# Last norm of a post-norm decoder layer: three quarter products moved behind the statistics, 44 idle products on TensorE, a register load pinned, the last output halves split

## The chip, the cores and the metric

The kernel runs on one core of one Trainium2 chip. The metric is the device time of one execution in microseconds (us), of which the median of several runs counts. The profile is that of one execution; its span runs from the first to the last instruction on the core.

## The reference, cut to what matters

One decoder layer over 256 tokens of width 1024. A mixer and a first layer norm come first and are not touched. Then a mixture of 16 experts, of which each token takes two, and the second layer norm, which is the end of the program:

```python
h = moe(x, w_router, router_bias, w_gate[l], w_up[l], w_down[l])
x = layer_norm(DN_ALPHA * x + h, ln2_g[l], ln2_b[l])

def layer_norm(x, g, b):
    mu = jnp.mean(xf, -1, keepdims=True)
    var = jnp.mean(jnp.square(xf - mu), -1, keepdims=True)
    y = (xf - mu) * lax.rsqrt(var + LN_EPS) * g + b
```

With y the row before the norm, r = 1/sqrt(var + eps) and m = -mu*r, the output is (y*g)*r + (m*g + b). The kernel computes y*g on VectorE, m*g + b as a small product on TensorE, and joins the two in one VectorE operation.

## The kernel before, in words

**Experts.** `moe_round` takes the 16 experts in eight pairs, numbered 0 to 7 in `pr`. For each pair the 64 token slots of each expert are multiplied by the gate and up weights (L1290), turned (L1361), and the pair before is multiplied by its down weights (L1301) and scattered back to the token rows (L1310, L1311) into four PSUM tiles `py` that gather all pairs. The weights come from HBM through a ring of buffers, issued on SyncE (L946). Pair 7 is the last: after its down weights have arrived nothing more is read from HBM.

**The last pair.** L1385 to L1390 handle the down product of pair 7 in four column quarters of 256. For each quarter: 16 products `pd` (L1301), a copy to a rounded part on ScalarE (L100) and the remainder on VectorE (L101), four scattering products `py` (L1310, L1311), the sum with the row, `y_sb` (L1377, one operation for each half of the tokens, n = 0 and 1), and the partial statistics (L1379). `last` calls `gained(i - 1)` first: the products y*g of the quarter before (L1270, two operations of 128x256).

**The branch.** Where some expert has more than 64 tokens, further rounds are needed. The count was put into an integer, and `nc.values_load` (L1351) loads it into a register of every engine. After `moe_round` each engine compares its register and branches (L1396): with the count at zero it goes through a short block, which waits on the engine's own semaphore and adds to it what the rounds left out would have added, and then jumps behind the loop's body, which holds one more copy of the experts' code. TensorE's part of that body is by far the longest.

**The last norm.** L1402 joins the statistics, L1404 takes the root on ScalarE, L1405 calls `gained(3, (0,))`, L1406 to L1410 make r and the columns of m, L1414 turns them with two TensorE transposes into `pn`, L1416 copies them to `nmT` on ScalarE, `gained(3, (1,))` follows. Then for each half c of the columns and each half n of the tokens: a product `pgb` of 5 rows by 512 columns (L1422, the first instruction that needs `nmT`), the joining operation `yo` (L1424), and the output transfer on SyncE's queue (L1425). L1449 is the end of the program, with its waits for the transfers.

**Order.** The order on each engine is a planner's, made ahead of time. `P` and `K` are one function, `keep_in_program_order`: it adds an edge to an instruction that puts it behind the instruction written just before it for the same engine. An instruction without the edge is placed where the planner likes, as far as its data allows. SyncE's order is that of the program. The register loads of L1351 have no edge. Each engine works through its instructions in order, TensorE's weight loads (PEld) aside, which run ahead of its products.

## Time and profile before

| | us |
|---|---|
| median of 3 runs | 617.74 (616.12 to 619.96) |
| the profiled execution | 617.43 |
| its span | 615.6 |
| granted TensorE clock, mean over the span | 0.989 |
| TensorE, products: busy | 587.5 (95%) |
| VectorE busy | 323.8 (53%) |
| ScalarE busy | 253.4 (41%) |

Of the profiled execution's 617.43 us, 1.8 us lie outside its span. The shares are averages over the whole span; the change lies in its last 2.5%, from about 600 us on, where TensorE is idle more than half of the time. [...]

### The profile page before, as it was taken

To read this page: it belongs to the slowest core of one execution; us is meant where nothing else is said; L and a number is where in the kernel's file an instruction comes from. 1 tells how busy PE (TensorE), PEld (TensorE's weight loads), DVE (VectorE), ACT (ScalarE), POOL (GpSimd) and SP (SyncE) were. 2 spreads that over 40 slices of the span, in tenths; PEclk is the share of its full clock that TensorE was granted. 3 is DMA by queue.
4 is the path that set the end of the run, shared out by engine and by line. 5 is a ranking of instruction groups with operands and counts; after the bars stand their busy time and mean duration, and the time that the engine had idled before them with its cause. 6 is when DMAs were issued, how large, how long until landed. Compare 5 with 4: busy or idle time off the path is not lost. (4 is left out here: it accounts for less than half of the span.)

```text
span 615.6 us, 10554 instructions
## 1 busy us (share of the span) xinstructions
PE 587.5 (95%) x4231; PEld 459.4 (75%) x4231; DVE 323.8 (53%) x651; ACT 253.4 (41%) x413; POOL 18.8 (3%) x53
## 2 busy tenths in 40 slices
PE   6999999999988999999999999999999999999992
PEld 5999999989978999999999999633533534444351
DVE  3798887677465986555565655542210300121245
ACT  5556664563469784443434544311211211021121
POOL 3000010100111000000000000000000000000000
PEclk9999999999999999999999999999999999999996
DMA  7877453742220436588998895889999999999941
GB/s 207 230 224 196 137 162 128 210 133 71 70 70 8 156 123 201 187 301 327 357 365 300 264 404 184 304 328 399 417 414 409 414 415 409 416 417 407 417 168 71
DMA packets 86380, 160.43 MB, mean 261 GB/s; under 512 B 9963, under 2 KB 56161, under 8 KB 86326
## 3 DMA queue, kind: packets, MB, share of 16 engines
q1 hardware_dynamic: 86198, 159.44, 71.5%
q8 instruction: 35, 0.57, 0.4%
q0 software_dynamic: 128, 0.26, 0.2%
q14 instruction: 19, 0.16, 0.1%
HBM read 158.50 MB, written 1.18 MB: 259 GB/s over the span
## 5 line engine op out<-in xcount | busy, mean ns | idle before, releaser
L133 DVE TENSOR_TENSOR wlo<-raw,whi 128x1024 fp32r<-128x1024 f32 (+1 forms) x106 | 125.9, 1200 | 53.3 <-ACT whi L129 52.6
L129 ACT CAST whi<-raw 128x1024 fp32r<-128x1024 f32 x102 | 105.9, 1048 | 101.4 <-PE pcm L275 34.8
L271 PE MATMUL pcm<-xh,whi 128*128 128x256 f32 x512 | 126.1, 284 | 2.3 <-ACT whi L131 1.5
L275 PE MATMUL pcm<-xl,whi 128*128 128x256 f32 x512 | 125.0, 282 | 0.0
L271 PEld LDWEIGHTS pcm<-xh,whi 128*128 128x128 f32 x512 | 97.4, 190 | 3.2 <-ACT whi L131 1.9
L275 PEld LDWEIGHTS pcm<-xl,whi 128*128 128x128 f32 x512 | 97.4, 190 | 0.1
L280 PE MATMUL pcm<-xh,wlo 128*128 128x256 f32 x512 | 72.5, 283 | 0.3 <-DVE wlo L133 0.2
L280 PEld LDWEIGHTS pcm<-xh,wlo 128*128 128x128 f32 x512 | 65.8, 190 | 0.8 <-DVE wlo L133 0.7
L101 DVE TENSOR_TENSOR dd<-pd,dd 128x512 fp32r<-128x512 f32 (+1 forms) x18 | 11.4, 632 | 95.3 <-ACT dd L100 95.3
L1301 PE MATMUL pd<-ew,sh 128*64 128x512 f32 (+1 forms) x288 | 56.8, 546 | 0.7 <-ACT sh L1362 0.7
L1290 PE MATMUL wu<-ew,xg 128*64 128x512 f32 x256 | 57.4, 593 | 0.0
L1290 PE MATMUL wg<-ew,xg 128*64 128x512 f32 x256 | 56.7, 595 | 0.6 <-issue 0.6
L1301 PEld LDWEIGHTS pd<-ew,sh 128*64 128x64 f32 x288 | 20.4, 137 | 35.1 <-issue 30.3
L1290 PEld LDWEIGHTS wu<-ew,xg 128*64 128x64 f32 x256 | 18.5, 137 | 36.2 <-issue 34.7
L1290 PEld LDWEIGHTS wg<-ew,xg 128*64 128x64 f32 x256 | 18.1, 137 | 33.5 <-issue 32.4
L271 PE MATMUL ptm<-whi,xh 128*128 128x256 f32 x128 | 32.6, 287 | 0.0
L271 PE MATMUL pbr<-yth,whi 128*128 128x256 f32 x128 | 32.1, 284 | 0.0
L275 PE MATMUL pbr<-ytl,whi 128*128 128x256 f32 x128 | 32.0, 282 | 0.0
L273 PE MATMUL ptm<-whi,xl 128*128 128x256 f32 x128 | 31.6, 281 | 0.0
L100 ACT CAST dd<-pd 128x512 fp32r<-128x512 f32 (+1 forms) x18 | 9.7, 539 | 46.3 <-PE pd L1301 46.3
L1207 ACT ACTIVATE xg<-pxg,gbp 128x128 f32<-128x128 f32 x32 | 13.3, 456 | 36.7 <-DVE xg L1206 35.8
L1341 DVE SCALAR_TENSOR_TENSOR sh<-wu,cw,sh 128x512 f32<-128x512 f32 x8 | 6.0, 751 | 37.9 <-PE wu L1290 37.8
(421 smaller groups left out, 887.5 us busy)
## 6 DMA issues: line engine op xcount, KB each, us to landing
raw<-in_w_in_dram SPq DMA_DIRECT2D x39, 1024.0 KB, 5.3
ew<-in_w_gate_dram SPq DMA_DIRECT2D x64, 512.0 KB, 9.8
ew<-in_w_up_dram SPq DMA_DIRECT2D x64, 512.0 KB, 9.6
ew<-in_w_down_dram SPq DMA_DIRECT2D x64, 512.0 KB, 9.8
raw<-in_w_branch_dram SPq DMA_DIRECT2D x8, 1024.0 KB
raw<-in_w_out_dram SPq DMA_DIRECT2D x4, 1024.0 KB
x<-in_x_dram SPq DMA_DIRECT2D x4, 256.0 KB, 5.3
raw<-in_w_in_dram SPq DMA_DIRECT2D x2, 512.0 KB
```

The lines of the kernel that those rows point to most:

```text
L100: A.copy(hi, ps)
L101: V.tensor_tensor(lo, ps, hi.bitcast(F32), op=OP.subtract)
L129: A.copy(hi, src)
L133: V.tensor_tensor(lo[:, c], src[:, c], hi[:, c].bitcast(F32), op=OP.subtract)
L271: T.matmul(o, sh(k), mh(k), start=first and k == 0, stop=False)
L273: T.matmul(o, sl(k), mh(k), start=False, stop=False)
L275: T.matmul(o, sh(k), ml(k), start=False, stop=False)
L280: T.matmul(o, sl(k), mh(k), start=False, stop=last and k == kt - 1)
L1207: A.activation(xg[1][:, 2 * kg + k, :], ps[kg][:, k, 128:256], AF.Identity, scale=g_, bias=b_)
L1290: P(T.matmul(p[r, :], xg[pr][:, k, r], W[pr, (nm, e, k // 2)][:, k % 2, :], start=k == 0, stop=k == 7))
L1301: P(T.matmul(p[r, :], hT[:, k, r], W[pr, ("wd", e, k)][:, 0, c0:c1], start=k == 0, stop=k == 3))
L1341: V.scalar_tensor_tensor(sg, pu, cw[pr // 2][:, pr % 2:pr % 2 + 1], sg, op0=OP.mult, op1=OP.mult)
```

## The change: what it does

Four edits. The product y*g of quarter 0 stays in `last`; those of quarters 1 and 2 leave it, and quarter 1 takes the place behind the statistics that quarter 3 had, with quarters 2 and 3 whole after the copy to `nmT`. Behind the last scattering product, 44 products of 128x256 in bfloat16 are added on TensorE; their result is never read. The second VectorE operation on the norm's weights in pair 7 gets the edge that keeps it behind the VectorE instruction written before it, which is that engine's register load. The last two of the four joining operations are cut in two halves of 256 columns, each with a transfer of its own.

```diff
-                    V.tensor_scalar(raw, raw, sgn[:, 1:2], None, op0=OP.mult)
+                    K(V.tensor_scalar(raw, raw, sgn[:, 1:2], None, op0=OP.mult))
...
         def last(c0, c1, dd, i):
 
-            if i:
-                gained(i - 1)
+            if i == 1:
+                gained(0)
...
         last(*cuts[-1], dd[0], len(cuts) - 1)
+        if first:
+            idle = pt("idle", (128, 2, 128))
+            for _ in range(44):
+                P(T.matmul(idle, selz[:, 1, 0:1].to_broadcast([128, 128]), stri[:, None, :].to_broadcast([128, 2, 128]),
+                           start=True, stop=True))
...
-    gained(3, (0,))
+    gained(1, (0,))
...
-    gained(3, (1,))
+    gained(1, (1,))
+    gained(2)
+    gained(3)
     for c in range(2):
         for n in range(2):
-            cs = slice(512 * c, 512 * c + 512)
             p = pt("pgb", (128, 512))
-            P(T.matmul(p, nmT[:, n, :], lnq[1][:, cs], start=True, stop=True))
-            y = yo[n][:, cs]
-            K(V.scalar_tensor_tensor(y, y, st2[:, n, 1:2], p, op0=OP.mult, op1=OP.add))
-            Q.dma_start(out[0, n * 128:(n + 1) * 128, cs], y)
+            P(T.matmul(p, nmT[:, n, :], lnq[1][:, 512 * c:512 * c + 512], start=True, stop=True))
+            for c0, c1 in ((0, 512),) if c + n < 2 else ((0, 256), (256, 512)):
+                y = yo[n][:, 512 * c + c0:512 * c + c1]
+                K(V.scalar_tensor_tensor(y, y, st2[:, n, 1:2], p[:, c0:c1], op0=OP.mult, op1=OP.add))
+                Q.dma_start(out[0, n * 128:(n + 1) * 128, 512 * c + c0:512 * c + c1], y)
```

## Rows read from the trace of the kernel before

**Rows 1.** The chain of waits that ended last, in order of time: start in us, length in us, what.

```profile
605.51 0.05 DVEq L1396
605.56 0.51 issue
606.07 0.40 DVE st L1402 x2
...
607.46 0.14 issue
607.60 0.60 PE pn L1414 x2
...
608.27 0.37 ACT nmT L1416
...
608.69 0.80 PE pgb L1422
...
609.51 0.89 DVE yo L1424 x2
```

**Rows 2.** VectorE's instructions in order of time: start, length, line and operation, out<-in and shapes, count; in brackets the idle time before and what ended it.

```profile
581.19 0.69 DVE L101 TENSOR_TENSOR dd<-pd,dd 128x512 fp32r<-128x512 f32 x1 [15.48 <-ACT dd L100]
...
600.98 0.75 DVE L1270 TENSOR_TENSOR yo<-y_sb,gall 128x256 f32<-128x256 f32 x2
...
601.65 0.75 DVE L1377 TENSOR_TENSOR y_sb<-py,y_sb 128x256 f32<-128x256 f32 x2
602.32 0.74 DVE L1379 BATCH_NORM_STATS2 bs<-y_sb 128x6 f32<-128x256 f32 x2
602.98 0.74 DVE L1270 TENSOR_TENSOR yo<-y_sb,gall 128x256 f32<-128x256 f32 x2
603.64 0.74 DVE L1377 TENSOR_TENSOR y_sb<-py,y_sb 128x256 f32<-128x256 f32 x2
604.30 0.74 DVE L1379 BATCH_NORM_STATS2 bs<-y_sb 128x6 f32<-128x256 f32 x2
606.07 0.39 DVE L1402 BATCH_NORM_AGGREGATE st<-bs 128x2 f32<-128x24 f32 x2 [1.03 <-DVEq L1396]
```

**Rows 3.** The register load and the branch by engine's sequencer: line, engine, operation, count, duration in ns as least/median/greatest, first and last start in us.

```profile
L1351 DVEq TENSOR_LOAD <-nmore x1: 544/544/544, 604.7 to 604.7; - x1
...
L1396 DVEq COMPARE_BRANCH  x2: 51/53/55, 605.3 to 605.5; - x2
...
L1396 ACTq COMPARE_BRANCH  x2: 38/44/49, 601.0 to 601.1; - x2
...
L1396 PEldq EVENT_SEMAPHORE  x1: 51/51/51, 601.8 to 601.8; - x1
...
L1396 PEldq COMPARE_BRANCH  x1: 3388/3388/3388, 601.9 to 601.9; - x1
```

**Rows 4.** The DMA view of the stretch 601 to 606 us: the traffic in 40 slices of 0.125 us, and the only queue that carried 16 KB.

```profile
GB/s 0 0 0 0 0 0 0 0 0 0 66 0 0 0 131 0 0 0 0 0 0 0 0 0 0 0 0 0 0 0 0 0 0 0 0 0 0 0 0 0
...
q8 instruction: 1, 0.02, 1.2%
```

**Rows 5.** TensorE's instructions in order of time (PE: products; PEld: weight loads), and last the weight loads of the scattering products from 590 us on as one group, with their mean in ns.

```profile
588.10 0.50 PE L1310 MATMUL py<-dd,ST 128*128 128x512 f32 x1
...
590.07 0.60 PE L1361 MATMUL pht<-ident,sh 128*128 128x128 f32 x4
...
595.22 0.28 PE L1311 MATMUL py<-dd,ST 128*128 128x256 f32 x1
595.34 0.28 PE L1310 MATMUL py<-dd,ST 128*128 128x256 f32 x1
595.46 0.28 PE L1311 MATMUL py<-dd,ST 128*128 128x256 f32 x1
...
601.47 0.28 PE L1311 MATMUL py<-dd,ST 128*128 128x256 f32 x1
607.60 0.58 PE L1414 MATMUL pn<-ident,nmc 128*5 128x128 f32 x2 [5.85 <-DVE nmc L1410]
608.69 2.07 PE L1422 MATMUL pgb<-gbr,nmT 5*128 5x512 f32 x4 [0.51 <-ACT nmT L1416]
...
L1310 PEld LDWEIGHTS py<-dd,ST 128*128 128x128 f32 x8 | 1.5, 188 | 1.2 <-issue 1.2
```

**Rows 6.** Stretches: us from and to, length, busy time of PE, PEld, DVE, ACT, POOL with their instructions, granted TensorE clock, DMA share, GB/s.

```profile
601.80:606.00 4.20, 0.00 (x0) 0.00 (x0) 3.24 (x10) 1.04 (x1) 0.00 (x0) 1.00 0.02 6
606.00:607.50 1.50, 0.00 (x0) 0.00 (x0) 1.27 (x8) 0.29 (x1) 0.00 (x0) 0.51 0.06 16
607.50:610.80 3.30, 2.65 (x6) 1.26 (x6) 1.57 (x3) 0.36 (x1) 0.00 (x0) 0.50 0.00 0
...
611.00:612.00 1.00, 0.00 (x0) 0.00 (x0) 1.00 (x2) 0.00 (x0) 0.00 (x0) 0.50 0.88 326
612.00:613.00 1.00, 0.00 (x0) 0.00 (x0) 0.24 (x1) 0.00 (x0) 0.00 (x0) 0.50 1.02 375
613.00:614.00 1.00, 0.00 (x0) 0.00 (x0) 0.00 (x0) 0.00 (x0) 0.00 (x0) 0.50 0.93 348
```

**Rows 7.** The joining operations and the output transfers: VectorE's four joins and, for comparison, four sums of the same width earlier, in order of time; SyncE's issue of the transfers (duration of one issue in ns, first and last start) and their time to landing.

```profile
588.91 2.47 DVE L1367 TENSOR_TENSOR y_sb<-py,y_sb 128x512 f32<-128x512 f32 x4
...
609.51 2.72 DVE L1424 SCALAR_TENSOR_TENSOR yo<-yo,st,pgb 128x512 f32<-128x512 f32 x4 [1.73 <-PE pgb L1422]
...
L1425 SPq DMA_DIRECT2D out_dram<-yo x4: 332/332/347, 610.3 to 612.3; - x4
...
DMA to landing us min/median/max: 2.2/2.2/2.2
```

## The prediction, made before the change was run

> **What bounds the kernel now.** Read first the granted clock and the busy shares: up to 600 us TensorE is the bound at full clock, and no edit touches that part except the pinned VectorE operation. So the question is the tail, and there the chain of waits is the view to read [rows 1]. It begins with VectorE's branch and runs through the join of the statistics, the transposes, the copy to `nmT`, the first `pgb` and the joining operations to the last transfer. Two things stand just outside the chain. VectorE worked without a gap up to the last partial statistics at 605.04 (604.30 + 0.74), and two of its pairs on the way are products y*g that the statistics don't need [rows 2]. And TensorE, idle since 601.75 (601.47 + 0.28), went through its own branch in that idle time: the wait on its semaphore at 601.8, then a jump that took 3.39 us, to 605.33 [rows 3]. It cost nothing, because the transposes' input came only at 607.46 [rows 1].

> **The products y*g.** Without quarter 1's pair the sum of quarter 2 starts 0.67 us sooner (601.65 - 600.98); its scattering products are done by then. Without quarter 2's pair, the same for quarter 3: 0.66. VectorE's last statistics end 1.33 sooner [rows 2]. What comes back behind the statistics: one operation in the place that quarter 3 had during the root (0), and five after the transposes' input, some 0.33 each (0.67 for two), 1.7 us. They lie beside transposes, copy and first `pgb`, which take 2.05 from 607.46 to 609.51 [rows 1]. Cover enough, and with a faster TensorE (1.5 us) they stick out by 0.1 to 0.2.

> **The register load.** On VectorE it stands at 604.7, behind all statistics, and takes 0.544 to 605.24; the second branch starts 0.27 later [rows 3]. Pinned, it falls into pair 7's stretch, where VectorE had waited 15.48 us before 581.19 [rows 2], so it costs nothing there; nothing queues behind it that is due, and no other engine waits for it. In its old place the wait for the last statistics (605.04) would then release the branch. On TensorE the branch began 0.19 after the last product's end (601.75 to 601.94), so VectorE's would begin at 605.23 in place of 605.51: a gain of 0.3. With the 1.33, the transposes' input comes at 605.85 instead of 607.46, **1.6 us sooner**.

> **The idle products.** Nothing like them is in the trace in bfloat16; the nearest rows are scattering products of the same 128x256, 0.117 us apart ((595.46 - 595.22) / 2) [rows 5]. [...] From above: the duration of a weight load, 0.188, if no load hid behind the product before it [rows 5]. I take 0.117, since these loads did hide. First one at 601.59, the 44th starts 43 x 0.117 = 5.03 later and ends at 606.90 (606.5 to 610.0).

> **What stands behind them.** The idle products are written ahead of the branch. TensorE's short block begins with a wait on its own semaphore, which before was met right when the last product had ended; the idle products count on that same semaphore. So the jump now starts 0.19 after 606.90, at 607.09, and takes its 3.39 where nothing hides it: TensorE is through at 610.48. That this is the price of the place and not of a busy chip, the DMA view bears out: in these 5 us one 16 KB piece was fetched on an instruction queue, 1.75 us into the stretch, within the jump [rows 4]. VectorE's and ScalarE's jumps cost 0.04 to 0.06 [rows 3], but VectorE then waited 0.51 for its next instruction [rows 1]. From the end of TensorE's jump to the first transpose the trace shows nothing; 0 to 0.51, and I take 0.14, what lay between input and transpose [rows 1]. First transpose at 610.62 in place of 607.60: **3.0 us later**, with the 1.6 us that VectorE won lying idle in front of it.

> [...]

> **The clock.** It was full until about 606.0, 4.2 us after the last product, and half for transposes and `pgb` [rows 6]. At half, the two transposes took 0.58 and the first `pgb` 0.80; at full clock four transposes take 0.60 and a first product of 512 columns 0.50 [rows 1, 5]. So full clock is worth about 0.2 at the transposes and 0.3 at `pgb`, 0.5 together. In my sum TensorE pauses 3.7 us before the transposes and 4.8 before `pgb`: less than the 4.2 for the first, more for the second. I take 0.2; ends 0 and 0.5.

> **The split output.** Four sums of 512 columns start 0.60 apart (2.47 less the last one's 0.68, over 3), two products of 256 columns 0.33: each half costs 0.03 more, 0.13 for four [rows 2, 7]. SyncE issues in 0.33, as fast as halves come. The last transfer is half as long, but from 611 to 614 the DMA share is 0.88 to 1.02, so 1 MB takes its 2.8 us whatever its cut [rows 6, 7]. At best 0.3 gained, at worst 0.2 lost; I take 0.

> **The sum.** 617.43, the profiled execution, + 3.0 - 0.2 + 0 = 620.2. That execution stands 0.31 below the median of 617.74, so the change comes to +2.8 on the one and +2.5 on the other; I predict **620.2 us**, 0.4% up. One per cent, 6.2 us, is about what a measurement of this kernel can tell from no change, so this is "within 1%".

> **Rival 1: the jump is not behind the idle products, or costs little** (chance 0.24). For it: only one jump of this kind is in the trace; 88 more TensorE instructions move its target against the 16 KB pieces, and its place may be loaded already. Against it: the body jumped over stays as long. With a jump of 0.05 TensorE is free at 607.28, 0.3 sooner than its transposes before, and 0.5 of clock on top: 616.6. If the jump doesn't wait at all, the transposes come 1.6 sooner, and the five products y*g end at 607.5, where the joins start in place of 609.51: 615.4. It decides from a jump of less than about 0.9 us on (616.6 reaches 617.4).

> **Rival 2: slower by more than forecast, the idle products run at the weight loads' pace** (0.06). Their stationary operand is one column read 128 times over, in a form the trace doesn't hold. At 0.188 they last 3.1 us longer: 623.3. Beyond 1% it comes from 0.20 each on. Against it: every load of 128x128 in rows 5 hid behind its product.

> **Rival 3: a second fetch** (0.05). A handful of TensorE instructions follow the jump; if they straddle two 16 KB pieces, TensorE stands again, for up to 3.4: 623.6. Before, the jump's target and the last `pgb` showed no such stop [rows 5].

> **How the numbers follow.** The forecast has 0.65. Its own range, with the idle products from 0.107 to 0.13, a start of 0 to 0.5, the clock and the split: 618.8 to 621.8. The range reaches down over rival 1, whose cases lie on the other side of no change: **615.5 to 622.0**; rivals 2 and 3 are left out. Faster by over 1% (under 611.5) needs 6 us, where all gains make 2.3: 0.02. Slower by over 1% (over 623.9) needs rival 2 or 3 at its dear end: 0.05. Within 1%: 0.93.

> **What would show it.** In the changed kernel's profile: VectorE's last statistics near 603.7 and its register load near 582; 44 products from 601.6 to 606.9; TensorE's semaphore wait right behind them and its jump again near 3.4; transposes near 610.6 with VectorE idle since 607.5; six transfers. I am wrong if the jump starts before the idle products end, or is short; then the transposes follow near 606 to 607.3 and the time is below 617.

## The result: 0.5% slower

The changed kernel takes 621.16 us (620.67 to 621.76, 6 runs), the kernel before 617.24 (614.54 to 619.96, 6 runs): a ratio of 1.0052, 95% interval 1.0029 to 1.0074. The forecast was 620.2, between 615.5 and 622.0.

Of 3.4 us more span in the profiled execution (619.0 against 615.6) the change made 2.3. To part the two, this section and the next count from the start of the last scattering product (L1311), up to which TensorE has the same work in both kernels: 601.47 in the kernel before [rows 5], 602.55 here. From there to the end of the span, the **tail**: 615.6 - 601.47 = 14.1 us before, 619.0 - 602.55 = 16.45 now (16.4 in the expectations below). The other 1.1 us came long before the change (last section).

The chain of waits of the changed kernel, in order of time; it answers to [rows 1]:

```profile
604.93 0.05 DVEq L1401
604.98 0.51 issue
605.49 0.40 DVE st L1407 x2
...
606.88 1.68 DVE yo L1270 x5
608.56 2.98 issue
611.54 0.39 PE pn L1419 x2
...
612.42 0.51 PE pgb L1428
```

The statistics are joined at 605.49, 2.9 us into the tail; in the kernel before it was 4.6. The input of the transposes is ready at 606.88, but they begin at 611.54. Between the two the chain can name nothing but the five products y*g, which the transposes don't need, and 2.98 us of "issue": waiting for nothing that the view shows. Who held them up stands in the sequencers' view, which answers to [rows 3] (a name with a q is an engine's sequencer; the branch is L1401 in this kernel):

```profile
L1401 ACTq COMPARE_BRANCH  x2: 38/44/49, 602.1 to 602.2; - x2
L1401 DVEq COMPARE_BRANCH  x2: 51/53/55, 604.2 to 604.9; - x2
L1401 PEldq COMPARE_BRANCH  x2: 95/1810/3525, 605.5 to 607.8; - x2
...
L1401 PEldq EVENT_SEMAPHORE  x1: 51/51/51, 607.7 to 607.7; - x1
```

and in TensorE's instructions in order of time, which answer to [rows 5]:

```profile
602.55 0.28 PE L1311 MATMUL py<-dd,ST 128*128 128x256 f32 x1
602.68 4.98 PE L1394 MATMUL idle<-stri,selz 128*128 128x256 bf16 x44
611.54 0.38 PE L1419 MATMUL pn<-ident,nmc 128*5 128x128 f32 x2 [3.88 <-issue]
612.42 1.65 PE L1428 MATMUL pgb<-gbr,nmT 5*128 5x512 f32 x4 [0.51 <-ACT nmT L1421]
```

The idle products end at 607.66 (602.68 + 4.98). The wait on TensorE's own semaphore is met at 607.7, the jump (the second of the two branches in its row; the first, 0.095 long, is the comparison) starts at 607.8 and takes 3.53, and 0.2 us after its end the transposes run. The same jump had run beside VectorE's statistics before; now TensorE (idle for 3.88 us up to the transposes) and VectorE (4.40 up to the joins) both stand still for it.

The granted clock was full up to the transposes and the first `pgb`. The stretches, as in [rows 6]:

```profile
606.00:607.50 1.50, 1.50 (x16) 1.23 (x13) 1.35 (x8) 0.21 (x1) 0.00 (x0) 1.00 0.02 5
607.50:610.80 3.30, 0.15 (x2) 0.00 (x0) 1.05 (x4) 0.00 (x0) 0.00 (x0) 1.00 0.02 5
610.80:612.00 1.20, 0.38 (x2) 0.12 (x2) 0.00 (x0) 0.00 (x0) 0.00 (x0) 1.00 0.00 0
612.00:613.00 1.00, 0.58 (x2) 0.48 (x3) 0.05 (x1) 0.36 (x1) 0.00 (x0) 0.97 0.05 16
613.00:614.00 1.00, 1.00 (x3) 0.33 (x1) 1.00 (x2) 0.00 (x0) 0.00 (x0) 0.50 0.00 0
```

Full clock for the transposes (0.38 for two, 0.58 before) and the first `pgb` (0.51, 0.80 before): 0.5 us gained, for 5 us of products and a jump laid open.

### The profile page after: what moved, and what is told of

Same layout as the page of the kernel before. It is cut to its first block, busy times and chain, and to the rows that moved or that the text cites. A ratio compares the mean times of both kernels' runs of the same rounds, so it can differ in the third digit from the quotient of the medians.

```text
span 619.0 us, 10646 instructions
## 1 busy us (share of the span) xinstructions
PE 592.6 (96%) x4275; PEld 464.6 (75%) x4275; DVE 324.1 (52%) x652; ACT 253.4 (41%) x413; POOL 18.9 (3%) x53
## 5 line engine op out<-in xcount | busy, mean ns | idle before, releaser
L101 DVE TENSOR_TENSOR dd<-pd,dd 128x512 fp32r<-128x512 f32 (+1 forms) x18 | 11.4, 632 | 95.3 <-ACT dd L100 95.3
L1290 PEld LDWEIGHTS wg<-ew,xg 128*64 128x64 f32 x256 | 18.1, 137 | 33.5 <-issue 31.8
```

The lines of the kernel that those rows point to most:

```text
L101: V.tensor_tensor(lo, ps, hi.bitcast(F32), op=OP.subtract)
L1290: P(T.matmul(p[r, :], xg[pr][:, k, r], W[pr, (nm, e, k // 2)][:, k % 2, :], start=k == 0, stop=k == 7))
```

## The experiments

Eight kernels, each read by its tail. The first was timed in 12 executions beside 17 of the kernel before; each of the others ran once, so its tail is a single reading. The clock at the transposes and at the first `pgb` (full or half) moves a tail by up to 0.5 (0.58 against 0.38, and 0.80 against 0.51). Times in us from the start of the last scattering product:

| kernel | transposes start | first `pgb` takes | tail |
|---|---|---|---|
| before | 6.1 | 0.80 | 14.1 |
| changed | 9.0 | 0.51 | 16.4 |
| changed, no idle products | 4.5 | 0.80 | 12.5 |
| before, idle products alone | 8.8 | 0.80 | 16.9 |
| changed, 88 idle products | 13.6 | 0.65 | 22.9 |
| changed, no branch | 4.9 | 0.50 | 12.4 |
| changed, no branch, no idle products | 3.7 | 0.80 | 11.5 |
| changed, no idle products, no pin | 4.8 | 0.80 | 12.8 |
| changed, no idle products, no cut | 4.5 | 0.81 | 12.3 |
| changed, 4 idle products behind the branch | 4.5 | 0.80 | 12.6 |

**Without the idle products.**

```diff
-        if first:
-            idle = pt("idle", (128, 2, 128))
-            for _ in range(44):
-                P(T.matmul(idle, selz[:, 1, 0:1].to_broadcast([128, 128]), stri[:, None, :].to_broadcast([128, 2, 128]),
-                           start=True, stop=True))
```

> The changed kernel without its 44 idle products. Tail = from the start of the last scattering product to the end of the span: 14.1 us in the kernel before, 16.4 in the changed one. Theory (the idle products hold up TensorE's jump, and nothing else in the change costs): TensorE is through its jump 3.9 us into the tail, the transposes start with their input at 4.5, at half clock as before; tail 12.3 to 12.6, so 1.5 to 1.8 us below the kernel before and near 4 below the changed one. Rival (the moved products or the cut output cost too): tail above 13.5.

Measured: tail 12.5 (614.2 - 601.72), and in time 616.38 us against 618.32, ratio 0.9968, interval 0.9952 to 0.9983 (618.32 is the kernel before, timed beside it). Faster than the kernel before by 0.3%. TensorE and its branch in this kernel:

```profile
601.72 0.28 PE L1311 MATMUL py<-dd,ST 128*128 128x256 f32 x1
606.19 0.58 PE L1414 MATMUL pn<-ident,nmc 128*5 128x128 f32 x2 [4.19 <-DVE nmc L1410]
```

```profile
L1396 PEldq COMPARE_BRANCH  x2: 95/1830/3565, 601.4 to 602.2; - x2
```

The jump is as long as ever, 3.57, but it starts at 602.2, and the transposes again wait for VectorE (`DVE nmc`), not for "issue". So the idle products alone turn a gain of 1.6 us into a loss of 2.3.

**The idle products alone**, put into the kernel before.

```diff
         last(*cuts[-1], dd[0], len(cuts) - 1)
+        if first:
+            idle = pt("idle", (128, 2, 128))
...
```

> The kernel before with the 44 idle products alone. Theory: TensorE's way (44 products, wait, jump) decides alone, VectorE's gains don't count: transposes 8.9 to 9.0 us into the tail as in the changed kernel, tail 16.4 to 17.0. Rival (the idle products cost a fixed 4 us wherever they stand, on top of VectorE's own time): 14.1 + 4 = 18.1.

Measured: tail 16.9 (618.3 - 601.39), with the transposes at 8.8 as in the changed kernel, where VectorE was 1.6 us sooner. The chain ends its wait in the same way:

```profile
607.39 0.34 DVE yo L1270
607.73 2.50 issue
610.23 0.60 PE pn L1419 x2
```

```profile
610.23 0.58 PE L1419 MATMUL pn<-ident,nmc 128*5 128x128 f32 x2 [3.74 <-issue]
```

VectorE's time does not enter: TensorE's way decides alone, and the rival's 18.1 is out. The 0.4 us over the changed kernel are the clock, which here had fallen before the transposes (0.60 and then 0.80 for the first `pgb`, in place of 0.39 and 0.51) after a pause no longer than there (3.74 against 3.88).

**88 in place of 44.**

```diff
-            for _ in range(44):
+            for _ in range(88):
```

> The changed kernel with 88 idle products in place of 44. Theory: each one costs its full 0.109 us, tail 16.4 + 4.8 = 21.2. Rival (some part of them still lies under VectorE's work or under the jump): below 20.

Measured: tail 22.9 (626.3 - 603.39), 1.7 above the theory. The transposes agree with it: 13.6 against 9.0, where 44 x 0.109 less 0.14 for a jump of 3.38 instead of 3.53 makes 4.66. The excess comes behind them:

```profile
617.03 0.38 PE L1419 MATMUL pn<-ident,nmc 128*5 128x128 f32 x2 [3.74 <-issue]
617.91 0.65 PE L1428 MATMUL pgb<-gbr,nmT 5*128 5x512 f32 x1 [0.51 <-ACT nmT L1421]
620.30 1.43 PE L1428 MATMUL pgb<-gbr,nmT 5*128 5x512 f32 x3 [1.74 <-issue]
```

Between the first and the second `pgb` TensorE stood for 1.74 us with its input there. From 613 to 621 us the DMA view counts two pieces on the instruction queue that brings 16 KB a piece (82 GB/s over 0.2 us), one in the jump (the eighth slice of 0.2 us, 614.4) and one at 617.6:

```profile
GB/s 0 0 0 0 0 0 0 82 0 0 0 0 0 0 0 0 0 0 0 0 0 0 0 82 0 0 0 0 0 0 0 0 0 0 0 0 338 369 379 226
...
q8 instruction: 2, 0.03, 1.9%
```

The changed kernel's own view, from 608 to 616 us, has two such pieces as well, one in the jump (608.6) and one at 612.0:

```profile
GB/s 0 0 0 82 0 0 0 0 0 0 0 0 0 0 0 0 0 0 0 0 82 0 0 0 0 0 0 0 0 0 0 0 72 348 399 369 369 410 358 369
...
q8 instruction: 2, 0.03, 1.6%
```

There all four `pgb` ran on. So the second piece is fetched in either kernel (in all eight profiles with the branch it starts 0.7 to 0.9 us after the jump's end), and new with 88 products is that TensorE stood still for 1.74 us, 0.8 to 1.0 us after that piece's start, as in the prediction's third rival. Why it did so here and not with 44, no run shows.

**Without the branch**, so without the further rounds for overfull experts and without the register loads, save SyncE's at 539.8 us; the idle products stay.

```diff
-    with tc.If(more[0] > 0, preferred_fallthrough_block=False):
-        with tc.For_i(0, more[0], 1):
-            V.tensor_scalar(rank, rank, -float(CAP), None, op0=OP.add)
-            moe_round({}, False, ([rings[0], (yp, "y", NY, NY)], NRA + NY))
```

> The changed kernel, idle products included, without the branch, so without the further rounds for experts with more than 64 tokens and without the register loads. Theory (the jump behind the idle products is the cost, not the products themselves): the transposes follow the last idle product, about 5.2 to 5.3 us into the tail, at full clock; tail 12.5 to 13.0. Rival (TensorE would be as late without a jump): tail 16 or more.

Measured: tail 12.4 (612.4 - 599.99), 4.0 less with the same 44 products:

```profile
600.11 4.98 PE L1394 MATMUL idle<-stri,selz 128*128 128x256 bf16 x44
604.93 0.38 PE L1414 MATMUL pn<-ident,nmc 128*5 128x128 f32 x2
605.76 1.19 PE L1423 MATMUL pgb<-gbr,nmT 5*128 5x512 f32 x4 [0.45 <-ACT nmT L1416]
```

The transposes follow the last product at once, in full clock. So the greater part of the cost is the wait and the jump behind the products; what their own length costs, the next run shows.

**Without the branch and without idle products:** the edits of the first and the fourth experiment together, on the changed kernel.

```diff
-            for _ in range(44):
...
-    with tc.If(more[0] > 0, preferred_fallthrough_block=False):
...
```

> The changed kernel without idle products and without the branch (no further rounds, no register loads). Without the branch the join of the statistics came 0.8 us sooner with idle products in place (2.15 against 2.94 us into the tail). Theory (without a jump the idle products cost only what of them sticks out behind the transposes' input, and their full clock pays part of it back): input at 3.5, transposes at 3.6 to 3.7, tail 11.4 to 11.9 against 12.45 with them. Rival (the full clock that the idle products keep is worth more than their length): tail above 12.45.

Measured: tail 11.5 (615.4 - 603.89).

```profile
607.56 0.38 PE L1409 MATMUL pn<-ident,nmc 128*5 128x128 f32 x2 [3.39 <-DVE nmc L1405]
608.39 2.07 PE L1418 MATMUL pgb<-gbr,nmT 5*128 5x512 f32 x4 [0.45 <-ACT nmT L1411]
```

Even with nothing behind them the 44 products cost 0.9 us net (12.4 - 11.5): the transposes come 1.3 us later with them (4.9 against 3.7), and the full clock returns 0.3 of that, at the first `pgb` (0.50 against 0.80).

**The pin taken back**, without idle products.

```diff
-                    K(V.tensor_scalar(raw, raw, sgn[:, 1:2], None, op0=OP.mult))
+                    V.tensor_scalar(raw, raw, sgn[:, 1:2], None, op0=OP.mult)
```

> The changed kernel without idle products and without the pinned operation, so that VectorE's register load may go back behind the statistics. Theory: the join of the statistics comes 0.3 us later (3.2 us into the tail in place of 2.94), tail 12.75 to 12.85 in place of 12.48. Rival (the load lies under the last statistics anyway): 12.5.

Measured: tail 12.8 (615.5 - 602.71), join of the statistics 0.33 later. VectorE's register load is back behind the statistics:

```profile
L1351 DVEq TENSOR_LOAD <-nmore x1: 545/545/545, 604.6 to 604.6; - x1
```

The pin is worth 0.3. What is left against the kernel before, 14.1 - 12.8 = 1.3, is the moved products, since the cut, which this kernel still has, is worth nothing (next run).

**The cut taken back**, without idle products.

```diff
-            for c0, c1 in ((0, 512),) if c + n < 2 else ((0, 256), (256, 512)):
+            for c0, c1 in ((0, 512),):
```

> The changed kernel without idle products and with the last output half in one piece. Theory (the transfers fill the DMA engines, a smaller last one gains nothing): tail 12.4 to 12.6, as with the cut (12.48). Rival (the smaller last transfer lands sooner): tail 12.8.

Measured: tail 12.3 (615.4 - 603.13).

```profile
607.60 0.38 PE L1414 MATMUL pn<-ident,nmc 128*5 128x128 f32 x2 [4.18 <-DVE nmc L1410]
```

The 0.2 less are the transposes, 0.38 here against 0.58, for no reason in the edit; from the first joining operation to the end it is 6.1 in both (615.4 - 609.31 and 614.2 - 608.10). The cut is worth nothing.

**Four idle products behind the branch** in place of the 44 ahead of it.

```diff
+    idle = pt("idle", (128, 2, 128))
+    for _ in range(4):
+        P(T.matmul(idle, selz[:, 1, 0:1].to_broadcast([128, 128]), stri[:, None, :].to_broadcast([128, 2, 128]),
+                   start=True, stop=True))
     pn = pt("pn", (5, 2, 128))
```

> The changed kernel with 4 idle products behind the branch, ahead of the transposes, in place of the 44 ahead of it. Theory: the jump starts 0.47 us into the tail as without them, they run from 4.2 to about 4.9 at half clock, too late to hold the clock through the jump; tail 12.5 to 12.9. Rival (a few products there keep the clock full): tail 12.0 to 12.2.

Measured: tail 12.6 (614.4 - 601.75).

```profile
605.75 0.75 PE L1414 MATMUL idle<-stri,selz 128*128 128x256 bf16 x4 [3.72 <-DVE st L1406]
606.29 0.63 PE L1418 MATMUL pn<-ident,nmc 128*5 128x128 f32 x2
```

```profile
605.50:606.00 0.50, 0.25 (x3) 0.25 (x4) 0.43 (x5) 0.00 (x0) 0.00 (x0) 1.00 0.00 0
606.10:606.60 0.50, 0.50 (x5) 0.23 (x2) 0.50 (x2) 0.00 (x0) 0.00 (x0) 0.50 0.11 33
```

They did not hold the clock: it fell from 1.00 to 0.50 while they ran, the two transposes took 0.63, and the four cost 0.1 us.

## Why the prediction was right, point by point

**Right in mechanism and size: the jump behind the idle products.** Predicted were idle products to 606.90, jump from 607.09 to 610.48, transposes at 610.62. In the changed kernel, with its 1.08 us of delay taken off (602.55 - 601.47), these are 606.6, 606.8 to 610.3 and 610.5. The two experiments that part the causes agree: without the products the jump is hidden again, without the branch the products cost little. Rival 1, with a jump that doesn't wait or is short, is out: the wait was met right behind the last product (607.66 and 607.7), and the jump took 3.53. VectorE's and ScalarE's branches took 0.04 to 0.06 again. TensorE's jump has a 16 KB piece in it in all eight profiles with the branch, and its length goes with the time of that piece (0.98 to 1.20 us of 3.37 to 3.61, last section). Whether the length of the body jumped over has a part in it, no run shows.

**Right: the products y*g and the pin.** 1.33 forecast, 1.3 measured; 0.3 forecast, 0.3 measured. That both lay idle in front of TensorE's jump is what the run with the idle products alone shows.

**Terms that were off.** The idle products were 0.109 apart, not 0.117: -0.35 over 43, so rival 2, at the weight loads' 0.188, is out; a load took 0.098 here. No run shows the 0.107 with which the lower ends of the forecast's own ranges were worked out (606.5 for the end of the last product, 618.8 for the time); the 44 products start from 602.7 to 607.4, which is 0.109 apart. The jump took 0.14 more. The clock held through the first `pgb` as well: -0.3 on the 0.2 taken. The prediction had chosen between the two by the length of the pause, and the pause does not decide it (last section). Together 2.8 - 0.35 + 0.14 - 0.3 = 2.3, which is the tail's 16.45 - 14.13.

**Wrong in the reading of the code, without a price: the cut.** The text ahead of the prediction and the prediction say that the last two joins are cut, with six transfers. The condition `c + n < 2` holds for three of the four; only the last one is cut, into five transfers. Its price was taken as 0 and is 0.

**Rival 3, a stop for a second fetch,** did not happen in the changed kernel, though the second piece was fetched there too; with 88 products TensorE did stop beside that piece, for 1.74 us. How near the changed kernel was to it, no run shows.

**The time.** 621.16 lies 1.0 above the forecast and 3.9 above the kernel before. The tail's 2.3 us, 0.4% of 617, lie inside the measured 0.3 to 0.7%. The rest of the 3.9 is not the predicted mechanism: in the profiled execution another 1.1 us came at 196 us, where the edits change nothing (last section); for the other executions it was not read. The forecast's own range adds up to 619.0 to 621.5 from the terms that the prediction names, not to 618.8 to 621.8; 621.16 lies in both.

## What to carry to other kernels

Before a gap of an engine is filled with work, look at what its sequencer does in that gap: here a jump of 3.39 us that cost nothing in the gap moved behind the filling, where it took 3.53 and nothing hid it. In this kernel TensorE's jump over the long body was best reached early (transposes at 4.5 in place of 9.0), with the products that weren't due left out; the version to keep here is the changed kernel without its idle products, at a ratio of 0.9968 (0.9952 to 0.9983) to the kernel before.

## What the runs showed of the hardware that was not expected

```profile
L1396 PEldq COMPARE_BRANCH  x2: 95/1850/3605, 602.8 to 603.6; - x2
```

```profile
q8 instruction: 1, 0.02, 5.4%
```

```profile
L1396 PEldq COMPARE_BRANCH  x2: 95/1732/3368, 601.4 to 602.2; - x2
```

```profile
q8 instruction: 1, 0.02, 4.4%
```

So the jump's end moves with the piece. About 0.9 of the other 2.4 us lie before the piece starts; what the remaining 1.5 behind it are, the traces don't show.

**The pause alone does not decide when the clock falls.** With the same 44 products and a pause of 3.9 us behind them the changed kernel kept full clock for the transposes; with a pause of 3.7 us the kernel before with idle products alone had lost it. Two kernels that differ only in the cut of the last output, both without idle products and with a pause of 4.2 us, had their transposes at half and at full clock. What decides was not tried.

**It falls in the middle of the kernel too.** In all ten profiles the granted clock is 0.79 over the stretch from 382 to 390 us, so the prediction's "full clock" up to 600 us is not quite so; this is the kernel before:

```profile
382.00:390.00 8.00, 6.62 (x40) 6.27 (x41) 4.72 (x30) 5.37 (x8) 0.00 (x0) 0.79 0.95 360
```

In the changed kernel's profile, not in that of the kernel before, TensorE has half clock in a stretch at 196 us as well, where the code is the same:

```profile
196.00:200.00 4.00, 3.47 (x17) 3.50 (x18) 3.96 (x13) 2.69 (x6) 0.00 (x0) 0.57 0.23 51
```

Five of the ten profiles show less than full clock there, and in these the last scattering product starts at 602.55 to 603.89, in the other five at 599.99 to 601.75. Laid beside the kernel before, instruction by instruction, the five lose 1.5 to 1.6 us between 190 and 202 us, and the others nothing; the changed kernel goes from 0.4 ahead to 1.2 behind and stays there. That is over half of the tail's 2.3, comes and goes without regard to the edit, and is why the tails were compared.
